# Where the output weights, the first pair's weights and the output operands of a hybrid flow step are made

## The chip, the cores and the metric

One core of one Trainium2 chip runs the whole step. The metric is the device time in microseconds. The core has five engines: PE (TensorE, matmul), DVE (VectorE), ACT (ScalarE), POOL (GpSimd) and SP, which here only issues DMAs. POOL issues some DMAs too. Each engine works through its own queue in order; semaphores order the engines against each other.

## The reference, cut to what matters

There is one layer and two groups of tokens: 2048 sample tokens and 128 prompt tokens, `D_MODEL` = 1024.

```
def mixer(xn, w_in, ..., w_branch, w_out, s0_f, s0_b, grid):
    proj = jnp.einsum('btd,de->bte', xn, w_in)
    qkv, beta, dec, z_a, u_b, v_b, z_b, x_c, z_c, gates = jnp.split(proj, points, axis=-1)
    qkv = short_conv(qkv, conv_w)
    ...
    br = jnp.stack([o_a, o_b, o_c], axis=2)          # delta scan, spatial gating, Fourier mix
    pb = jnp.einsum('btnw,nwd->btnd', br, w_branch)
    gt = jax.nn.sigmoid(gates.reshape(B, T, N_BRANCH, D_MODEL))
    merged = jnp.einsum('btnd,btnd->btd', gt, pb)
    return jnp.einsum('btd,de->bte', merged, w_out), s_f, s_b

def reference(...):
    shift, scale, gate = ada_mod(c, w_ada[l], b_ada[l])
    ...
    h = h + gate * out                               # then a final rmsnorm
```

## The kernel before

Tokens lie along the free axis, channels on the partitions. A value that a matmul reads is held as a pair of f16 halves, a high and a low part, after scaling by a power of two; a product then takes three matmuls (high·high, high·low, low·high). Making such a pair (`as_pair`, L933 to L935, or `converting`, L305 to L330) takes a scaled copy on ACT for the high half and a multiply and subtract on DVE for the low one. The scale comes from a sum of squares: ACT squares and sums along the free axis, DVE narrows that to bf16, PE sums it over the partitions with a matrix of ones (`wscb`), and DVE makes the exponent with integer operations (L279 to L281). `mm` (L251) issues every matmul, so nearly all of PE's work has this one line.

The step runs in stages. The framework puts the instructions of each engine in order by priorities and a simulation of its own; `tc.high_priority` and `tc.issue_after` influence it.

1. From the start to about 190 us the tokens are normed and turned, and the normed tokens xh and xl stay in SBUF.
2. From about 190 to 490 us, the conv stage: twelve tiles of 128 qkv columns, each a product over blocks of up to 512 tokens (L1011 to L1025), then a three-tap convolution in three long DVE operations over 2178 columns (L1031 to L1033), SiLU and a store. Beside it run the decays of the delta scan (L923, L924 on DVE), paced, and a generator `beside`, three steps of it after each 512-token block. `beside` first makes the `token_sums`, sums and differences of quarters of the normed tokens as f16 pairs, stored to DRAM for the last merge; then `out_w`: for each of four pairs of column blocks of the output matrix it squares, scales and splits the blocks into f16 pairs `slot` (stored as `wo`), and makes four differences of the blocks (`ot`, on POOL), split likewise and stored as `tw`.
3. From about 500 to 1100 us the scan is prepared and the branches B and C are made.
4. From about 1100 to 1784 us, two merges (`merge`, branches 1 and 2). Per 128 output channels and token block: 24 gate matmuls, 12 branch matmuls, a sigmoid on ACT, products on DVE and, in the second merge, an addition on POOL. The delta scan itself is paced beside them, and so is `gate_rows`: sums for the two residual gate rows, 64 DVE operations (L478, L480) on loads of `w_ada`, stepped by `next(gates, 0)`.
5. From about 1784 to 2047 us, the last merge, of branch 0. It works on pairs of output channel blocks (i and i + 4) and on quarters of the tokens by a scheme of seven products in place of eight, in two passes over the tokens with four pairs each. Its weights come from `pair_weights`: for each pair it loads two blocks of gate weights (`wst`) and the branch weights, squares them in the first pass for the scale, forms differences on POOL, and splits all into `whi`, `wlo`, `bhi`, `blo`. In the second pass all this but the scale is done afresh. `upto(u)` runs the parts that are due at a product u of the pair before. The branch values of branch 0 are `o16`, in a tile named `big`, [128, 2, 4, 2176] f16, loaded in f32 pieces `st` and split. Each pair's merged rows are also turned into seven-fold operands of the output product and stored to DRAM (`paD`, tile `pa` in pool `orp`, L1929).
6. From about 2047 us, the output products: the prompt's (`whole`), then eight pairs of token tiles (`two_tiles`), also with seven products for eight, each on an operand `pa` of 1792 KB loaded from `paD` and on the weights `wo` and `tw`, which lie in the space of xh and xl by then. The loads stand on SP behind each other by `in_turn` (L2182).

Pools matter at two places. The pool `orp` of the last merge is opened where the pools of the merges are closed, and the pool of the output stage where `orp` is closed; a tile in the new pool waits for all that used the space before. `wp` holds the weights in work: two tiles `wst`, four each of `whi` and `wlo`.

Of the kernel before, what the change touches and what calls it, by code (L numbers as in the profile page):

```python
# [20 lines left out]
P = 128  # L21
D = 1024
# [173 lines left out]
def hybrid_flow_kernel(ctx: ExitStack, tc: tile.TileContext, x_prompt, x_sample, state_delta, c, c_ctx, w_ada,  # L196
# [48 lines left out]
    newest, gated_, queued = [None], [None], [False]  # L245
# [59 lines left out]
    def converting(w, st, nkt, cols=P, hi=None, lo=None, tag="w", bufs=5, nth=0):  # L305
# [13 lines left out]
        sb16 = widened(ss, wp, "wsc")  # L319
        if wnext[0] < 11:  # L320
            yield
        s, inv = scales(None, wp, "wsc", sb16)
        w.inv = sb(wp, [P, 1], "winv", bufs=10)
        if isx is None:
            w.own = inv
        else:
            V.tensor_mul(w.inv, inv, isx)
        yield
        w.made = A.activation(w.hi, st, AF.Copy, scale=s)
        w.low = V.scalar_tensor_tensor(w.lo, st, s, w.hi, ALU.mult, ALU.subtract)  # L330
# [612 lines left out]
    q4 = slice(0, 4), slice(4, 8)  # L943
    tp = pool(a1, "tp", 1, side="right")
# [22 lines left out]
    def out_w():  # L967


        for j in range(4):  # L970
            sts = [sb(tp, [P, KT, P], "osts", bufs=2) for _ in range(2)]
            for st, i in zip(sts, (j, j + 4)):
                SY.dma_start(st, w_outb[i].rearrange("p (k c) -> p k c", c=P))
            yield 1
            yield 1
            yield 1
            ss = sb(tp, [P, 2], "oss2", bufs=2)
            for i in range(2):
                A.activation(sb(tp, [P, KT, P], "slot", F16, bufs=4), sts[i], AF.Square, accum_out=ss[:, i:i + 1])
                yield 1  # L980
            sb16 = sb(tp, [P, 1], "oss2b", BF16, bufs=2)
            V.tensor_add(sb16, ss[:, 0:1], ss[:, 1:2])
            yield 1
            s, inv = scales(None, wp, "wsc", sb16)
            for i in (j, j + 4):
                V.tensor_copy(winv[:, i:i + 1], inv)
            yield 1

            def put(dst, src):
                slot = sb(tp, [P, 2, 4, P], "slot", F16, bufs=4)  # L990
                as_pair(slot[:, 0], slot[:, 1], src, s)
                SY.dma_start(dst, slot.rearrange("p l k c -> p l (k c)"))
# [12 lines left out]
    def one_by_one(*gens):  # L1005
        for gen in gens:
            yield from gen
# [1407 lines left out]
```

## Time and profile before

| | us |
|---|---|
| median of three runs | 2244.32 (2244.15 to 2245.19) |
| the profiled execution | 2239.06 |
| its span | 2237.3 |
| PE busy | 2085.7 |
| DVE busy | 1493.8 |
| ACT busy | 1115.0 |
| POOL busy | 978.7 |

The span is what the profile shows from the first instruction to the last; the profiled execution's own time is 1.8 us longer. Busy times count instructions in work. A row of a group shows the line, the engine, the operation, what it writes and reads, its count, then its busy time and mean, and behind the second bar the idle time of its engine just before it with what ended it. PE's clock is shown as a share of full speed; after a long pause matmuls run slower for a while, and the row shows it.

### The profile page before, as it was taken

The page shows a single profiled execution, that of the slowest core. Times are in us where ns is not written, and L with a number is a line of the kernel's source. Part 1 is how long each engine was busy: PE and PEld are TensorE (multiplying, and loading weights), DVE is VectorE, ACT ScalarE, POOL GpSimd, SP SyncE. Part 2 cuts the span into 40 slices and gives each one's busy share as a digit, 9 for nine tenths or more (in the row PEclk, how much of TensorE's full clock was granted, in tenths as well). Part 3 has the DMA queues.
Part 4 walks back from the last instruction along what each step waited for, and adds up shares of the span by engine and source line. Part 5 has one row for each costly group of instructions (what it writes and reads, how often), then busy time and mean ns, then how long its engine had stood idle before and what let it go on. Part 6 is the DMA issues. An engine that isn't in the chain of part 4 may idle for free.

```text
span 2237.3 us, 43354 instructions
## 1 busy us (share of the span) xinstructions
PE 2085.7 (93%) x16169; PEld 1192.7 (53%) x16169; DVE 1493.8 (67%) x3056; ACT 1115.0 (50%) x2545; POOL 978.7 (44%) x1170
## 2 busy tenths in 40 slices
PE   8998888989999999989899999999999889996997
PEld 4454434445555587668556555555555445442443
DVE  6669996668876776665765566766654376885345
ACT  5554655656565564354544445655554354442112
POOL 0345664444565655533422223354452246553364
PEclk9999989999999999999999999999999999998999
DMA  8534864547777574343655556767654743842862
GB/s 351 198 107 135 258 238 145 200 136 231 248 249 243 181 237 119 85 136 112 199 178 168 162 180 189 239 217 222 213 182 154 244 160 135 299 141 110 331 226 85
DMA packets 250467, 427.54 MB, mean 191 GB/s; under 512 B 46200, under 2 KB 133008, under 8 KB 247184
## 3 DMA queue, kind: packets, MB, share of 16 engines
q1 hardware_dynamic: 197744, 323.68, 45.0%
q0 software_dynamic: 12688, 57.04, 6.8%
q10 hardware_dynamic: 39824, 44.05, 5.9%
q8 instruction: 127, 2.08, 0.4%
q14 instruction: 84, 0.69, 0.1%
HBM read 273.46 MB, written 151.22 MB: 190 GB/s over the span
## 4 chain that ended last, share of the span: by engine, by line
PE 42%; DVE 10%; DMA 8%; issue 4%; ACT 4%; POOL 3%; SPq 0%; ACTq 0%; POOLq 0%; DVEq 0%
PE b L251 41%; DMA st<-br 2%; DMA wst<-in_w_blk_dram 1%; DMA wst<-in_w_ada_dram 1%; DVE pa L935 1%; DMA br<-o 1%; POOL E L1201 1%; DVE XB L1200 1%; DMA ei<-XB 1%; DVE wlo L935 1%; DMA pa<-pa 1%; DMA N<-n 1%; DVE wlo L330 0%; POOL mr L2080 0%; DVE big L1786 0%
## 5 line engine op out<-in xcount | busy, mean ns | idle before, releaser
L251 PE MATMUL b<-xh,wlo 128*128 128x512 f16 (+2 forms) x1792 | 599.8, 347 | 17.0 <-DVE wlo L330 17.0
L251 PE MATMUL b<-xh,whi 128*128 128x512 f16 (+2 forms) x1792 | 602.5, 347 | 6.6 <-ACT sg L2090 3.1
L251 PE MATMUL b<-xl,whi 128*128 128x512 f16 (+2 forms) x1792 | 603.0, 347 | 0.0
L251 PEld LDWEIGHTS <-whi 128*128 128x128 f16 x3872 | 348.7, 98 | 334.4 <-issue 24.8
L251 PEld LDWEIGHTS <-wlo 128*128 128x128 f16 x1936 | 189.7, 98 | 200.0 <-DVE wlo L330 18.7
L251 PE MATMUL b<-big,bhi 128*128 128x512 f16 (+1 forms) x960 | 253.2, 350 | 2.9 <-ACT big L1785 1.2
L251 PE MATMUL b<-big,blo 128*128 128x512 f16 (+1 forms) x480 | 163.2, 348 | 0.0
L251 PEld LDWEIGHTS <-xh 128*128 128x128 f16 x1512 | 119.5, 98 | 34.0 <-issue 4.4
L251 PEld LDWEIGHTS <-bhi 128*128 128x128 f16 x960 | 86.9, 98 | 90.5 <-issue 18.2
L1201 POOL TENSOR_TENSOR E<-E,XB 128x31 f32<-128x31 f32 (+15 forms) x155 | 94.3, 609 | 77.3 <-DVE XB L1200 62.0
L1274 POOL COPY T<-ES 32x256 f16<-32x256 f16 x68 | 31.3, 460 | 202.5 <-DMA ES<-ei 193.2
L251 PE MATMUL b<-xh,pa 128*128 128x512 f16 x376 | 100.7, 383 | 20.1 <-DMA pa<-pa 20.1
L251 PEld LDWEIGHTS <-pa 128*128 128x128 f16 x648 | 63.8, 99 | 98.4 <-issue 23.3
L251 PE MATMUL b<-whi,xh 128*128 128x128 f16 x544 | 93.7, 220 | 2.0 <-DVE sg L1542 2.0
L251 PE MATMUL b<-whi,xl 128*128 128x128 f16 x544 | 93.6, 220 | 0.0
L251 PE MATMUL b<-wlo,xh 128*128 128x128 f16 x544 | 93.6, 220 | 0.0
L1825 POOL TENSOR_TENSOR mrow<-mrow,sg 128x512 f32<-128x512 f32 (+1 forms) x40 | 48.4, 1210 | 83.0 <-DVE sg L1824 62.6
L1381 POOL TENSOR_TENSOR skn<-skn,ed 128x512 f32<-128x512 f32 x34 | 37.1, 1090 | 107.9 <-DMA skn<-kv 94.9
L1037 POOL TENSOR_TENSOR cy<-cy,raw 128x545 f32<-128x545 f32 (+1 forms) x48 | 65.1, 1382 | 43.6 <-ACT raw L1036 43.6
L1200 DVE TENSOR_TENSOR XB<-XB,E 128x31 f32<-128x31 f32 (+15 forms) x155 | 54.6, 353 | 41.8 <-POOL E L1201 40.9
L251 PEld LDWEIGHTS <-xl 128*128 128x128 f16 x824 | 74.5, 98 | 14.4
L251 PE MATMUL b<-xl,pa 128*128 128x512 f16 x272 | 77.2, 382 | 0.0
(565 smaller groups left out, 4825.3 us busy)
## 6 DMA issues: line engine op xcount, KB each, us to landing
wst<-in_w_blk_dram SPq DMA_DIRECT2D x66, 512.0 KB, 4.3
pa<-pa POOLq DMA_DIRECT2D x16, 896.0 KB, 4.5
pa<-pa SPq DMA_DIRECT2D x8, 1792.0 KB, 7.7
qkv<-cy POOLq DMA_DIRECT2D x12, 1089.0 KB, 4.9
st<-br SPq DMA_DIRECT2D x48, 256.0 KB, 3.3
dc<-dec SPq DMA_DIRECT2D x17, 512.0 KB, 4.4
kq<-qkv SPq DMA_DIRECT2D x34, 256.0 KB, 5.1
kv<-tok POOLq DMA_DIRECT2D x17, 512.0 KB, 5.2
```

What stands on the lines that cost most here:

```text
L251: newest[0] = PE.matmul(out, l, r, start=start, stop=stop, skip_group_check=reopened)
L935: V.scalar_tensor_tensor(lo, src, s, hi, ALU.mult, ALU.subtract)
L1037: G.tensor_tensor(y[:, c0:c1], y[:, c0:c1], raw[:, 1 + c0:1 + c1], ALU.mult)
L1200: V.tensor_tensor(t3, X3[:, 0:k, k:k + 1].to_broadcast([P, k, n_]), E3[:, k:k + 1, k:32].to_broadcast([P, k, n_]), ALU.mult)
L1201: G.tensor_tensor(E3[:, 0:k, k:32], E3[:, 0:k, k:32], t3, ALU.subtract)
L1274: G.tensor_copy(T16[rows(a0, b), :, :, b], ES[0:32, :, 2 * a0 + b, :, wT])
L1381: G.tensor_tensor(h3(kn_), h3(kn_), bc(ed[:, d, t, :], P), ALU.mult)
L1825: G.tensor_tensor(mr, mr, sg, ALU.add)
```

## The change

- `out_w` leaves the conv stage. It is now a generator `weights_out` stepped in the merges: after each token block from the second channel block of the first merge on (`step=`), and in `norm_step` in the second. It has a pool of its own (`wop`), makes the block differences in place, and takes its squares behind the newest gate product's sigmoid.
- In `token_sums` the splits are a plain copy on ACT and a subtraction, in turn on POOL and on DVE. Each block now advances it by two steps.
- `urgently()` puts the parts of a weight conversion at high priority during the conv stage.
- `gate_rows` leaves the merges for the second pass of the last merge, every second product of its first three pairs.
- The first pair's weights of the last merge are begun in the second merge's last channel block, a part after each token block (`due_`), in the pool `wq`, which is not that of the merges. It was `orp`.
- In the first pass each pair's converted halves are stored to DRAM (`wgD`, `wbD`); in the second they are loaded (`stored`) and not made again.
- The output operands no longer have three buffers. Operands 0, 3, 6 lie in token columns 1024 to 1920 of `o16`, 1, 4, 7 in columns 0 to 896, and 2 and 5 in a tile `pa`. The first is loaded after the second pass's first pair, when that pass works on the other tokens. The sums `tw` are loaded in the last pair.

On PE, around the end of the second merge, before (`bsums` and `wscb` are summed over the partitions for the scales of branch weights and of gate weights; `whi` and `bhi` are high halves of gate and branch weights):

```order
L251 MATMUL b_23758<-big_14010,bhi_23329 128x128
L251 LDWEIGHTS blo_23330
L251 MATMUL b_23758<-big_14010,blo_23330 128x128
L251 LDWEIGHTS ones_2_89
L251 MATMUL b_23817<-bsums_2925_23815,ones_2_89 128x27
...
L251 MATMUL b_23847<-wscb_23845,ones_2_89 128x1
L251 LDWEIGHTS bhi_23873
L251 MATMUL b_24045<-big_14010,bhi_23873 128x512
...
L251 MATMUL b_24155<-big_14010,bhi_23873 128x512
```

The sum for the first pair's scale stands behind all of the merge, and branch matmuls follow it. The same place now, with the row of that sum ahead of it:

```order
L254 MATMUL b_23539<-big_13781,blo_23213 128x512
...
L254 MATMUL b_23556<-wscb_23554,ones_2_89 128x1
L254 LDWEIGHTS whi_23154
L254 MATMUL b_23578<-xh_94,whi_23154 128x512
...
L254 MATMUL b_23672<-big_13781,blo_23213 128x128
L254 LDWEIGHTS ones_2_89
L254 MATMUL b_23739<-bsums_2910_23737,ones_2_89 128x27
L254 LDWEIGHTS whi_23620
L254 MATMUL b_23789<-xh_94,whi_23620 128x64
...
L254 MATMUL b_23789<-xl_95,whi_23620 128x64
```

That sum has moved up 146 rows, into the merge, and gate products follow `bsums`. On SP, the loads at the passage from the last merge to the output, before (`room` holds rows of x, `tw` the weight differences):

```order
L2165 DMA wst_26262<-gate 128x1024
...
L2182 DMA room_26274<-in_x_prompt_dram 128x512
L2182 DMA pa_3208_26283<-pa 128x4x1792
L2182 DMA xh_94<-tw 128x4x1024 x2
L2182 DMA xl_95<-tw 128x4x1024
L2182 DMA room_26274<-in_x_sample_dram 128x1024 x2
L2182 DMA xl_95<-tw 128x4x1024
L2182 DMA pa_3209_26291<-pa 128x4x1792
```

The first operand stands behind the first use of `room`. And now, with the load of the first operand from the second pass:

```order
L2200 DMA big_13781<-pa 128x4x896 x2
...
L1935 DMA whi_26034<-wg 128x512
L1935 DMA wlo_26035<-wg 128x512
L2190 DMA xh_94<-tw 128x4x1024
L2190 DMA xl_95<-tw 128x4x1024
L2190 DMA xh_94<-tw 128x4x1024
L2190 DMA xl_95<-tw 128x4x1024
L2190 DMA room_26261<-in_x_prompt_dram 128x512
L2190 DMA room_26261<-in_x_sample_dram 128x1024 x2
L2190 DMA big_13781<-pa 128x4x896 x2
```

The first operand and `tw` have moved ahead of `room`; the second operand follows it.

```diff
+    def urgently():
+        return tc.high_priority() if urgent[0] else ExitStack()
...
-        with behind_gate():
+        with behind_gate(), urgently():
             w.squared = A.activation(w.lo, st, AF.Square, accum_out=ss)
...
                     st = sb(ep, [P, 2, cn], "st", F16, bufs=3)
-                    as_pair(st[:, 0], st[:, 1], f, 1.0)
+                    A.copy(st[:, 0], f)
+                    (V if i % 2 else G).tensor_tensor(st[:, 1], f, st[:, 0], ALU.subtract)
                     SY.dma_start(sD[p_][:, i, :, k, :], st)
...
-    beside = one_by_one(token_sums(), out_w())
+    beside = token_sums()
...
-                    for _ in range(3):
+                    for _ in range(2):
                         next(beside, 0)
...
-    big = pool(ms_, "big", 1)
+    big = pool(ctx, "big", 1)
     bwp.append(pool(mr_, "bwp", 1))
+    wop = pool(mr_, "wop", 2)
...
-                if each is not None or db > 3:
-                    next(gates, 0)
...
+    def out_w():
+        for j in range(4):
...
+            ss = sb(wop, [P, 2], "oss2")
+            for i in range(2):
+                with tc.issue_after(gated_[0].ins):
+                    A.activation(sb(wop, [P, KT, P], "slot", F16), sts[i], AF.Square, accum_out=ss[:, i:i + 1])
+                yield 1
...
+            b11, b21, b12, b22 = [st[:, q] for st in sts for q in halves]
+            for q, out, x, y in ((0, b11, b12, b11), (2, b12, b22, b12), (1, b22, b22, b11), (3, b21, b21, b22)):
+                G.tensor_tensor(out, x, y, ALU.subtract)
+                yield 1
+                put(tD[q, :, j, :].rearrange("p (l x) -> p l x", l=2), out)
...
-    inv_ = merge(1, True, inv_, then=(2, 20))
+    inv_ = merge(1, True, inv_, then=(2, 20), step=lambda db: next(weights_out, 0) if db else 0)
...
+            wq_.append(pool(last_s, "wq", 1, side="right"))
             sums_in(1)
+            cur.append(pair_weights(0, False))
...
+    due_ = [9, 6, 5, 4, 3, 1]
+
     def norm_step(db):
-        if db > 1 and early:
+        if db == KT - 1:
+            cur[0].upto(due_.pop())
+        if next(weights_out, 0):
+            return
+        if early:
...
+        def stored(self, i):
+            pair = lambda: [sb(wp, [P, KT, P], n_, F16, bufs=4) for n_ in ("whi", "wlo")]
+            ...
+            for due, w_, names in ((3, 0, ("b11", "t2")), (5, 1, ("b21", "t3")), (8, 2, ("t1", "t4")), (10, 3, ("b22",))):
+                yield due
+                ts = pair()
+                for l in range(2):
+                    SY.dma_start(ts[l][:, 0:4 * len(names)], wgD[i, w_, l][:, 0:512 * len(names)].rearrange("p (k c) -> p k c", c=P))
...
+            def keep(w_, ts, nk=KT):
+                for l in range(2):
+                    SY.dma_start(wgD[i, w_, l][:, 0:nk * P], ts[l][:, 0:nk].rearrange("p k c -> p (k c)"))
...
+    def own(i):
+        if i % 3 == 2:
+            return operands(opa, "pa")
+        t0 = (1024, 0)[i % 3]
+        return o16[:, :, :, t0:t0 + 7 * P].rearrange("p l k (n c) -> p k l n c", c=P)
...
     for n_, (p_, i) in enumerate(order):
         nxt = pair_weights(order[n_ + 1][1], n_ > 2) if n_ < 7 else None
...
+            if 3 < n_ < 7 and u % 2 == 0:
+                next(gates, 0)
+            if n_ == 7 and u == 0:
+                gates_in()
+            if n_ == 7 and u in (4, 6):
+                for q in ((1, 0), (2, 3))[u == 6]:
+                    sums_of(q)
...
+        if nxt is not None:
+            nxt.upto(99)
...
+        if n_ == 4:
+            next_pair()
...
     in_turn(x_left, xp_[0:P, left])
-    next_pair(in_turn)
-    sums_of(1)
-    sums_of(2)
-    sums_of(0)
     ahead_rows = two_rows(firsts[0], in_turn)
-    sums_of(3)
     next_pair(in_turn)
```

More of the change, by code (lines that the diff above doesn't have):

```diff
@@ L942, in hybrid_flow_kernel @@
     winv = sb(cp, [P, KT], "winv8")
-    q4 = slice(0, 4), slice(4, 8)
-    tp = pool(a1, "tp", 1, side="right")
+    halves = slice(0, 4), slice(4, 8)
+    urgent[0] = True
     def token_sums():
@@ L1894, in hybrid_flow_kernel @@
     inv_ = merge(2, False, inv_, finish_delta, then=(0, 17), step=norm_step)
-    for _ in gates:
-        pass
     while wsteps:
@@ L1949, in hybrid_flow_kernel @@
     gp, last_load = [], []
-    halves = slice(0, 4), slice(4, 8)
     bscale = sb(cp, [P, 4 * KT], "bscale")
```

282 lines of the change are left out of this document (146 added, 136 removed).

## The prediction

> **What bounds the kernel now.** I read the page's busy shares first, then PE's waits stage by stage, then the windows of the worst stages, then the timeline around the two longest waits. The page's first part gives the busy time of each engine:
>
> ```profile
> span 2237.3 us, 43354 instructions
> PE 2085.7 (93%) x16169; PEld 1192.7 (53%) x16169; DVE 1493.8 (67%) x3056; ACT 1115.0 (50%) x2545; POOL 978.7 (44%) x1170
> ```
>
> TensorE (PE) is busy for 2085.7 of 2237.3 us. So all that this change can win without removing matmuls is 151.6 us of idle time, and a little of PE's own time where matmuls run at half clock after a wait. The waits of PE by line show where that time is: 350 to 500 us and 250 to 350 us (the conv stage), 1770 to 1840 us (merge 2 to the last merge) and 2035 to 2090 us (the last merge to the output products); columns: line waited for, us in all, times, longest.
>
> ```profile
> PE b L251 <- DVE wscb L265: 7.7, 1, 7.7
> PE b L251 <- DVE oss2b L982: 2.9, 1, 2.9
> ...
> PE b L251 <- DVE wlo L330: 17.0, 3, 6.5
> ...
> PE b L251 <- DVE wscb L1990: 12.2, 1, 12.2
> PE b L251 <- DMA mr<-mrg: 0.8, 1, 0.8
> ...
> PE b L251 <- DMA pa<-pa: 20.1, 1, 20.1
> ```
>
> Two single waits, 12.2 and 20.1 us, and a stage with 27.6 us in three kinds of wait (17.0 + 7.7 + 2.9). The windows (busy us and instruction count of PE, PEld, DVE, ACT, POOL, then granted clock, DMA share, GB/s) show what the conv stage lacks, and that the merges and the last merge have little to give:
>
> ```profile
> 250.00:300.00 50.00, 39.65 (x185) 17.86 (x186) 50.00 (x45) 28.97 (x40) 24.08 (x18) 0.90 0.77 260
> 300.00:350.00 50.00, 43.54 (x231) 20.69 (x230) 40.87 (x64) 28.36 (x51) 31.22 (x41) 0.93 0.54 179
> 350.00:400.00 50.00, 42.27 (x225) 20.16 (x224) 34.31 (x57) 29.39 (x51) 17.89 (x20) 0.90 0.48 163
> ...
> 1500.00:1550.00 50.00, 47.21 (x428) 28.08 (x427) 32.04 (x79) 26.02 (x76) 23.52 (x31) 1.00 0.68 209
> ...
> 1950.00:2000.00 50.00, 50.00 (x233) 22.70 (x232) 43.84 (x55) 23.50 (x36) 25.41 (x21) 1.00 0.40 137
> ```
>
> From 250 to 300 us DVE is busy for all 50.00 us: there DVE is the bound, and PE waits for its low halves (wlo). From 350 us DVE has 15.7 us free and the stage waits for single chains instead.
>
> **Conv stage.** Two things leave it: the whole of out_w, and half of the subtractions of the token sums go from DVE to POOL; and token sums advance two steps per block, not three. The groups of 200 to 500 us (count, busy us, mean ns, idle before), and in the last row what SP's queue waited for at the stores of slot (330 to 480 us):
>
> ```profile
> L935 DVE SCALAR_TENSOR_TENSOR st<-sg,st 128x512 f16<-128x512 f32 (+1 forms) x32 | 21.1, 673 | 7.9 <-ACT st L934 7.9
> L935 DVE SCALAR_TENSOR_TENSOR slot<-ot,wsc,slot 128x512 f16<-128x512 f32 x16 | 14.4, 914 | 11.1 <-ACT slot L934 11.0
> L935 DVE SCALAR_TENSOR_TENSOR slot<-osts,wsc,slot 128x512 f16<-128x512 f32 x16 | 12.9, 857 | 2.1 <-ACT slot L934 2.1
> ...
> L924 DVE TENSOR_TENSOR dc<-dc,cst 128x1024 f32<-128x1024 f32 x8 | 13.5, 1683 | 0.0
> ...
> L924 DVE TENSOR_TENSOR E<-E,cst 128x1024 f32<-128x1024 f32 x3 | 3.6, 1211 | 0.0
> ...
> L957 POOL TENSOR_TENSOR sg<-sg,sg 128x512 f32<-128x512 f32 (+1 forms) x8 | 17.7, 2214 | 10.7 <-DVE sg L956 10.5 <-DVE bnds L1482 0.2
> L1001 POOL TENSOR_TENSOR ot<-osts,ot 128x512 f32<-128x512 f32 x7 | 14.7, 2105 | 5.0 <-DVE slot L935 5.0
> ...
> SPq L992 <- DVE slot L935: 44.3, 18, 17.0
> ```
>
> The gain splits at about 340 us. Before it: half of 21.1 us, 10.6 us, leaves DVE, and the rest is thinner per tile of 128 qkv columns. By the starts of the first conv tap (L1031), such a tile takes 25.2, 31.9 and 26.1 us, in the three that four starts bound; PE's own part, three matmuls for each of eight K tiles and of 4.25 blocks, is 22 us at the 0.216 us between the starts of two warm matmuls of 512 columns (the last two rows, from another stage).
>
> ```profile
> 223.78 2.25 DVE L1031 TENSOR_SCALAR cy<-raw,pc 128x2178 f32<-128x2178 f32 x1
> ...
> 248.95 1.34 DVE L1031 TENSOR_SCALAR cy<-raw,pc 128x2178 f32<-128x2178 f32 x1
> ...
> 280.81 1.34 DVE L1031 TENSOR_SCALAR cy<-raw,pc 128x2178 f32<-128x2178 f32 x1
> ...
> 306.91 2.24 DVE L1031 TENSOR_SCALAR cy<-raw,pc 128x2178 f32<-128x2178 f32 x1
> ...
> 2051.69 0.38 PE L251 MATMUL b<-xh 128*128 128x512 f16 x1
> 2051.91 0.38 PE L251 MATMUL b<-xl,xh 128*128 128x512 f16 x1
> ```
>
> That is 3 + 10 + 4 = 17 us beyond PE's part, the 17.0 of the waits. Moving 10.6 us of DVE work pays at most 10.6 there; the order still puts two or three long conv taps between the parts of one weight conversion, so I take half, 5. After 340 us the 7.7 and 2.9 us go whole if their causes go: oss2b is a row of out_w, and the wscb wait is the last link of a weight load that stands in SP's queue, which stood 44.3 us before stores of slot. I take 10. Together −15, bounds 0 (the chains of 350 us on were not SP's doing, and POOL's new subtractions return the rest) and −28 (all 27.6).
>
> What speaks against it is POOL. The same DVE subtraction of 1024 columns takes 1.21 us in one group above and 1.68 us in another, and POOL's 2.21 us: I read this as the two engines slowing each other. The change puts 16 subtractions on POOL and takes out_w's away (14.7 us for seven of them), so the overlap stays about equal; that is why I give no loss. The Trainium skill, "SBUF — State Buffer", section "Who interferes with whom", states that a DVE instruction with two SBUF inputs contends with a GpSimd instruction that reads SBUF. By it each moved subtraction that meets a DVE tensor_tensor would hand back what it saved, and this term would be −10 rather than −15; the two durations of L924 agree with it.
>
> **Start of the last merge.** Before, the first pair's weights may only be squared when merge 2's pools have been given back: its last merged row (mrow) is stored, then ACT squares, DVE adds, PE sums.
>
> ```profile
> 1783.67 0.18 PE L251 MATMUL b<-bsums,ones 128*128 128x27 bf16 x1
> 1796.00 0.16 PE L251 MATMUL b<-wscb,ones 128*128 128x1 bf16 x1 [12.15 <-DVE wscb L1990]
> 1796.99 2.72 PE L251 MATMUL b<-big,bhi 128*128 128x512 f16 x6 [0.82 <-DMA mr<-mrg]
> ...
> 1792.66 1.06 ACT L1987 ACTIVATE wt<-wst 128x1024 f16<-128x1024 f32 x1 [1.28 <-DMA mrg<-mrow]
> ```
>
> In the changed order of PE, shown with the change, the sum wscb stands 146 rows before bsums, in merge 2, and right behind bsums stand gate products, which need nothing of the branch. So 12.15 + 0.82 us go. The six matmuls at 1796.99 come 0.43 us apart against 0.216 later (2.72 us for six, the last of them overlapping): about 1.3 us of half clock also goes. I take back 1 us for a first wait on the converted block: −13, bounds −14.3 and −10 (a first wait as long as one 512 KB load, 4.3 us; its row stands under C).
>
> **Start of the output.** The first output operand (pa) waits for the pool that the last merge holds, which the last store of pa gives back:
>
> ```profile
> 2052.12 0.38 PE L251 MATMUL b<-xh,xl 128*128 128x512 f16 x1
> 2072.58 0.59 PE L251 MATMUL b<-xh,pa 128*128 128x512 f16 x1 [20.08 <-DMA pa<-pa]
> ...
> 2076.80 0.38 PE L251 MATMUL b<-xl,pa 128*128 128x512 f16 x1
> ...
> 2058.88 4.10 DMA pa<-pa
> ...
> 2063.37 0.33 SPq L2182
> ...
> 2063.75 8.05 DMA pa<-pa
> ...
> 2067.88 3.64 SPq L2182 DMA_DIRECT2D room<-in_x_sample_dram  x2
> ```
>
> In the changed order of SP (shown with the change) the first pair's operand is loaded 47 rows before the sums tw, among the second pass's loads, into a finished token range of the branch operand's buffer; the sums tw stand before room. The first pair of output tiles can follow the prompt's products at once: −20.1, and −2.1 for ten matmuls that start 4.22 us apart from first to last, at half clock, where 2.16 is the warm time. What is late next is the second operand. It still stands behind room, which still waits for the last pa store: at 2063.37. With 0.33 us for room's issue and 3.64 for the two loads of x it is issued at about 2067, and its 8.05 us end at about 2075, its first half some us before. Were nothing else to change, PE would have used up the prompt's part at 2052.3 and the first pair, an eighth of the output's 142.1 us on PE, 17.8, at 2070. So some 4 us of the wait come back; −22 + 4 = −18, bounds −22 (the loads overtake) and −10 (the second operand and x share the bandwidth and take 8 us more).
>
> **Merges and passes.** Added to the merges: out_w, that is 8 squares and 32 conversions on ACT, 32 on DVE at 0.9 us as above, 16 blocks on POOL at up to 2.1 us, 8 loads and 32 stores on SP. Taken away: the gate rows, whose DVE work is
>
> ```profile
> L480 DVE SCALAR_TENSOR_TENSOR sg<-wst,scT,sg 128x256 f32<-128x256 f32 x56 | 26.4, 517 | 11.0 <-DMA wst<-in_w_ada_dram 10.9
> ```
>
> so DVE's sum there is level (14.4 + 12.9 = 27.3 against 26.4), and it is free for a third of that stage. In the second pass the pairs' conversions, 14 loads instead of them, free DVE from its 43.84 of 50 us; PE has 0.0 idle in that window, so this wins nothing. The price is the order of the queues: a store waits on SP for its conversion, with the next loads behind it. Bounds −6 (the idle 2.8 us of a merge window, twice) to +12 (one more wait like that of 12.15); no row stands nearer to one end, so I take the middle, +3.
>
> **Sum.** −15 − 13 − 18 + 3 = −43. The profiled execution took 2239.06 us around its span of 2237.3; that gives 2196, and the three runs shown have their median 5.3 us above it, so 2201. I say 2202.
>
> **Rivals.**
> A. The conv stage gives nothing: POOL's subtractions hold up DVE where DVE is full, or the long taps set the pace in any case. For it: 50.00 of 50 us, and the order, in which weight conversions are still spread between taps. Against: 27.6 us named waits, of which 10.6 hang on out_w alone. 2202 + 15 = 2217; if they give back only the first part's 5, 2207.
> B. It gives all: 2202 − 13 = 2189. For it: DVE has room from 300 us on. Against: the 17.0 us come with a DVE that stays nearly full.
> C. Slower. In the second pass each of four pairs now takes four groups of weights from DRAM through SP's queue, together with gate rows, merged rows and the first operand. The DMA part of the page has a load of this size, 512 KB, at 4.3 us to landing:
>
> ```profile
> wst<-in_w_blk_dram SPq DMA_DIRECT2D x66, 512.0 KB, 4.3
> ```
>
> If SP's first-in order makes every one of the 16 groups late by its whole landing, 16 × 4.3 = 69 us are lost: 2271. It decides from ten of 16 groups, where 43 us are gone. Against: four buffers per half, so a group can be two ahead, and a DMA share of 0.40.
> D. Nothing in the balance: the waits move, the first to the branch's operand (the first six matmuls' big), the second to the second pa, and the conv stage stays as in A. That gives 2244, the change doing what it says without time to show. For it: the last store of pa still releases room at the same moment. Against: by the order only the second operand stands behind it.
>
> **Numbers.** My forecast 0.53, A 0.20, B 0.12, D 0.06, C 0.09. The range goes from below B, at the lower bounds of the two other terms (2189 − 13 = 2176), to the forecast with all three gains at their small ends and the last term at its large one, nearly (2202 + 15 + 3 + 8 + 9 = 2237): 2176 to 2236. It leaves out D and most of C and so some 0.15. A measurement here tells 0.2% (4.5 us) from no change. Faster takes the forecast, A and B, 0.85; within 0.2% D, 0.06; slower C, 0.09.
>
> **What would show it.** Conv: the three waits gone or at most 10 us in 250 to 500 us. Last merge: no wait over 3 us near its start, with gate products right behind bsums. Output: no wait between the prompt's last matmul and the first on an operand, and one of some 4 us on the second operand 18 us later. Merges and passes: PE's waits there as small as before; waits on whi or wlo from DRAM of several us in the second pass would be C. I am wrong if the time is above 2236.

## The result and the profile after

The changed kernel takes 2210.96 us (median of four, 2209.05 to 2213.18), the kernel before 2244.76 us beside it (2244.15 to 2246.48). The ratio is 0.9849, with a 95% interval of 0.9831 to 0.9866: 34 us or 1.5% faster, where 42 us were forecast. The profiled execution has a span of 2207.3 us against 2237.3, 30.0 us less. Its page, part 1, after the change:

```profile
span 2207.3 us, 43369 instructions
PE 2084.7 (94%) x16169; PEld 1194.0 (54%) x16169; DVE 1445.0 (65%) x3000; ACT 1096.3 (50%) x2513; POOL 982.1 (44%) x1178
```

PE does the same work in the same time (2084.7 us against 2085.7), so 29 of the 30 us are idle time of PE. Where they went is read off four marks that both traces have; each is the start of one instruction:

| mark | before, us | after, us | won in the stretch up to it | forecast for it |
|---|---|---|---|---|
| first tap of the last conv tile | 468.40 | 468.21 | 0.2 | 15 |
| sum for the branch scales (bsums) | 1783.67 | 1777.17 | 6.3 | -3, for merges and passes together |
| first matmul of the prompt's output | 2047.16 | 2037.87 | 2.8 | 13 |
| end of the span | 2237.3 | 2207.3 | 20.7 | 18 |

The sum of the forecast, 43, was 13 too high on this scale. Its parts missed by 2.7 to 14.8 us each, two one way and two the other. The main waits of PE in the changed kernel, 150 to 250 us, 250 to 350, 1750 to 1840, 1840 to 2010 and 2030 to 2210 us (us in all, times, longest):

```profile
PE b L254 <- DVE wscb L268: 6.1, 2, 3.4
...
PE b L254 <- DVE wscb L268: 26.9, 4, 10.8
...
PE b L254 <- DVE sg L1789: 2.1, 1, 2.1
PE b L254 <- DVE wscb L1958: 1.3, 1, 1.3
...
PE b L254 <- ACT sg L2128: 3.4, 2, 3.0
PE b L254 <- DVE st L2076: 3.3, 2, 2.8
...
PE b L254 <- DMA big<-pa: 1.6, 2, 0.9
```

Both long single waits are gone, the 20.1 us on an operand nearly whole: 1.6 us are left of it. So are all three waits of the conv stage, 27.6 us, but others of 33.0 us stand before 350 us. They are of a kind of which the kernel before had one of 7.7 us, after 350 us: PE waits for wscb, the narrowed sum of squares of a weight block. After 350 us only 1.1 us are left. The windows show in which half (columns as before):

```profile
200.00:250.00 50.00, 43.92 (x225) 21.25 (x224) 50.00 (x40) 29.40 (x40) 28.62 (x17) 0.93 0.69 237
250.00:300.00 50.00, 37.35 (x203) 17.99 (x202) 50.00 (x42) 30.19 (x40) 37.62 (x26) 0.90 0.67 234
300.00:350.00 50.00, 35.75 (x168) 16.05 (x167) 42.44 (x52) 29.21 (x52) 43.39 (x46) 0.86 0.44 148
350.00:400.00 50.00, 49.09 (x269) 23.78 (x268) 22.39 (x33) 20.34 (x36) 14.49 (x25) 1.00 0.34 118
```

From 350 us PE is nearly full (49.09 of 50 us). Before that it lost what it wins there: 117.0 us busy in 200 to 350 us, against 133.0 before. DVE stays full, and POOL has become busier in 300 to 350 us (43.39 of 50 us, before 31.22).

### The profile page after: what moved, and what is told of

Same layout as the page of the kernel before. It is cut to its first block, busy times and chain, and to the rows that moved or that the text cites. A ratio compares the mean times of both kernels' runs of the same rounds, so it can differ in the third digit from the quotient of the medians.

```text
span 2207.3 us, 43369 instructions
## 1 busy us (share of the span) xinstructions
PE 2084.7 (94%) x16169; PEld 1194.0 (54%) x16169; DVE 1445.0 (65%) x3000; ACT 1096.3 (50%) x2513; POOL 982.1 (44%) x1178
## 4 chain that ended last, share of the span: by engine, by line
PE 59%; DVE 15%; DMA 11%; issue 5%; ACT 4%; POOL 4%; SPq 1%; ACTq 0%; POOLq 0%; DVEq 0%
PE b L254 55%; PE b L183 3%; DMA wst<-in_w_blk_dram 2%; DMA st<-br 1%; DMA wo<-slot 1%; DMA sqk<-qk 1%; DVE xl L183 1%; POOL E L1167 1%; DVE pa L941 1%; PE b L1068 1%; DVE cy L997 1%; DVE st L970 1%; DMA ES<-ei 1%; DVE XB L1166 1%; DVE cy L998 1%
## 5 line engine op out<-in xcount | busy, mean ns | idle before, releaser
L1002 POOL TENSOR_TENSOR cy<-cy,raw 128x545 f32<-128x545 f32 (+1 forms) x48 | 70.1, 1486 | 90.6 <-ACT raw L1001 90.6
L254 PEld LDWEIGHTS <-big 128*128 128x128 f16 x480 | 46.8, 98 | 59.4 <-DMA big<-pa 2.6
L254 PE MATMUL b<-xh,big 128*128 128x512 f16 x280 | 74.8, 379 | 1.6 <-DMA big<-pa 1.6
L960 POOL TENSOR_TENSOR sg<-xh,xl 128x512 f32<-128x512 f16 (+1 forms) x36 | 59.2, 1648 | 35.3 <-DVE st L970 14.9
```

Of the source, the lines that this page charges most:

```text
L254: newest[0] = PE.matmul(out, l, r, start=start, stop=stop, skip_group_check=reopened)
L960: on.tensor_tensor(f, xh[:, kk, ts], xl[:, kk, ts], ALU.add)
L1002: G.tensor_tensor(y[:, c0:c1], y[:, c0:c1], raw[:, 1 + c0:1 + c1], ALU.mult)
```

## The experiments

Each kernel is the changed one with the edit shown, unless another is named. A ratio is to the kernel before, timed beside it on the same chip; the changed kernel has 0.9849 (0.9831 to 0.9866). A difference of 0.001 is 2.2 us, and two ratios tell apart what differs by some 0.0025 or more. "Conv mark" is the start of the last tile's first tap: 468.40 us before, 468.21 after. Five kernels below (m_gates, l_remake2, p0_late, p0_orp, o_late) leave the conv stage as the change made it, and their marks lie between 467.8 and 468.9, so a difference of some us there is more than chance. "First six tiles" is the time from the first tile's first tap to the seventh's.

### The conv stage: subtractions shared with POOL

```diff
-                    A.copy(st[:, 0], f)
-                    (V if i % 2 else G).tensor_tensor(st[:, 1], f, st[:, 0], ALU.subtract)
+                    as_pair(st[:, 0], st[:, 1], f, 1.0)
```

> The changed kernel with the token sums' splits as before: every subtraction on DVE, none on POOL. If POOL's subtractions slow DVE down where it is full (contention theory), the first six conv tiles, 157.1 us in the changed kernel, come back to about 153 as before or below, and the whole is some 4 us faster than the changed kernel. If the sharing helped and something else fills DVE (load theory), about 8 us of DVE work come back to the first half and it takes some 160 to 165, the whole up to 6 us slower.

This is c_dve. Ratio 0.9822 (0.9801 to 0.9843), whose interval overlaps the changed kernel's, span 2197.4 us. The first six tiles take 150.9 us, and the conv mark is at 458.99: 9.2 us earlier. It is the answer of the contention theory, and twice its size. More work on DVE made the stage shorter. Groups of 200 to 340 us, kept apart by size, first of the changed kernel, then of this one (where the taps stand one line earlier):

```profile
L997 DVE SCALAR_TENSOR_TENSOR cy<-raw,pc,cy 128x2178 f32<-128x2178 f32 x6 | 17.6, 2928 | 0.0
L998 DVE SCALAR_TENSOR_TENSOR cy<-raw,pc,cy 128x2178 f32<-128x2178 f32 x5 | 14.3, 2869 | 0.0
L970 DVE TENSOR_TENSOR st<-sg,st 128x512 f16<-128x512 f32 x9 | 11.1, 1244 | 0.0
L966 DVE TENSOR_TENSOR sg<-sg,sg 128x512 f32<-128x512 f32 x4 | 5.5, 1382 | 0.0
L965 DVE TENSOR_TENSOR sg<-sg,sg 128x512 f32<-128x512 f32 x4 | 2.7, 666 | 0.0
...
L970 POOL TENSOR_TENSOR st<-sg,st 128x512 f16<-128x512 f32 x8 | 15.4, 1931 | 7.2 <-ACT st L969 7.2
```

```profile
L997 DVE SCALAR_TENSOR_TENSOR cy<-raw,pc,cy 128x2178 f32<-128x2178 f32 x6 | 17.3, 2884 | 0.0
L996 DVE SCALAR_TENSOR_TENSOR cy<-raw,pc,cy 128x2178 f32<-128x2178 f32 x6 | 15.9, 2647 | 0.0
L941 DVE SCALAR_TENSOR_TENSOR st<-sg,st 128x512 f16<-128x512 f32 x16 | 15.3, 967 | 0.0
L966 DVE TENSOR_TENSOR sg<-sg,sg 128x512 f32<-128x512 f32 x3 | 3.0, 994 | 0.0
L965 DVE TENSOR_TENSOR sg<-sg,sg 128x512 f32<-128x512 f32 x3 | 2.9, 955 | 0.0
```

The means go up in some rows (the splits' subtractions 1244 ns against 967, L966 1382 against 994) and down in others (L965 666 against 955), because each is a mixture of two durations. In both traces every one of the 24 sums of 512 columns on DVE (L962, L965, L966) takes either 0.62 to 0.69 us or 1.51 to 1.66 us, and every long one overlaps work of POOL. So what counts is how many operations POOL's work hits. From 150 us to the seventh tile's first tap, 63 of DVE's 193 operations in the changed kernel last over 0.25 us longer than the shortest of their kind, and 51 of 218 here; each of them overlaps work of POOL. By the same measure DVE loses some 59 us to this in the changed kernel and 48 here, an estimate from the two timelines. That takes back most of what leaves DVE: it is busy 185.3 us of that stretch in the changed kernel and 184.4 here. Besides, it stands idle 23.4 us there in the changed kernel and 15.1 here, mostly waiting for ACT's copies and POOL's sums. POOL also stands in the changed kernel's chain of work that ended last, where it had other work to do for the convolution:

```profile
245.72 6.64 POOL sg L960
252.36 2.16 POOL st L970
254.52 6.77 POOL cy L1002 x4
```

The prediction gave this sharing no loss, because out_w's POOL work left the stage too. But out_w's blocks stood after 340 us, where DVE had room; the subtractions came to stand at 200 to 340 us, where it has none. The Trainium skill, "SBUF — State Buffer", section "Who interferes with whom", says that a DVE instruction with two SBUF inputs contends with a GpSimd instruction that reads SBUF; the two durations of the sums, 0.68 and some 1.63 us, the long one only beside POOL, agree. How the 9.2 us divide between that and the waits for ACT and POOL, no run tells apart.

### The conv stage: the priority of a weight conversion

```diff
-    urgent[0] = True
```

> The changed kernel without high priority for the parts of a weight conversion in the conv stage. If the priority is what made PE wait for scale sums (26.9 us on wscb in 250 to 350 us) in place of low halves (17.0 us before), those 26.9 us fall to under 17 and the first six tiles to 150 or less. If DVE's load is the cause, the wait changes its name only, and the six tiles stay within 3 us of 157.

This is c_calm. Ratio 0.9812 (0.9791 to 0.9833), span 2196.0 us, conv mark at 457.69: 10.5 us earlier. Of the expectation's two sides neither holds whole. The wait on wscb did fall away (26.9 to nothing in 250 to 350 us, where 8.0 us on wlo stand instead, with 9.3 more on wlo in 200 to 250), but the first six tiles take 161.2 us; they start 5 us earlier, and the tiles after them win nearly 10. The taps are DVE's work; PE itself is busy 131.4 of the 150 us from 200 to 350 us, against 117.0 in the changed kernel. What the priority did is seen in PE's timeline of the changed kernel:

```profile
252.17 0.38 PE L254 MATMUL b<-xh,wlo 128*128 128x512 f16 x1
252.38 0.38 PE L254 MATMUL b<-xh,whi 128*128 128x512 f16 x1
263.53 0.16 PE L254 MATMUL b<-wscb,ones 128*128 128x1 bf16 x1 [10.77 <-DVE wscb L268]
263.56 0.59 PE L254 MATMUL b<-xl,whi 128*128 128x512 f16 x1
263.94 0.63 PE L254 MATMUL b<-xh,wlo 128*128 128x512 f16 x1
```

A sum of one column, for a tile to come, stands in the midst of a group of products that have all their operands. PE takes its queue in order, so the whole of PE waits 10.77 us for a DVE cast of 0.14 us that is late behind other DVE work, and then runs at half clock (0.43 us from one start to the next, 0.216 before the wait) until 266.8. "Urgent" moved the sum ahead in PE's queue, and not what it waits for. The squares on ACT end at 253.74 us; the cast starts at 263.34, behind six DVE operations that run from 253.43 us on. These take 10.4 us, all beside work of POOL, where the shortest of their kinds add up to 4.6, so this one wait holds a part of POOL's price too.

### The conv stage: both, and the number of steps

c_only undoes the two and also takes three steps again; of the change's edits to the conv stage, only the removal of out_w is left. c_both leaves two steps.

```diff
-    urgent[0] = True
-                    A.copy(st[:, 0], f)
-                    (V if i % 2 else G).tensor_tensor(st[:, 1], f, st[:, 0], ALU.subtract)
+                    as_pair(st[:, 0], st[:, 1], f, 1.0)
-                    for _ in range(2):
+                    for _ in range(3):
```

> The changed kernel with the conv stage as before in all but the output weights: splits on DVE, three steps a block, no high priority for weight conversions; only the output weights' scaling has left it. By the prediction's term the 10.6 us of waits that hung on them go, and the last first-tap starts at about 458, the whole 8 to 12 us faster than the changed kernel, like each of the two single undoings (459.0 and 457.7 there). If the two undoings add, it starts at about 449 and the whole is 16 to 20 us faster. If both only happened to give a better order, it can be anywhere, 468 too.

> The changed kernel with splits on DVE and no high priority for weight conversions, but the change's two steps a block where the kernel that gave ratio 0.9755 has three. If the number of steps is of no account, the last first-tap starts within 3 us of 448.1 and the ratio is 0.974 to 0.977. If two steps thin the load out, the first six tiles take under 150 us and the ratio is below 0.974; if they only move the order, it can be up to 0.981.

c_only: ratio 0.9755 (0.9738 to 0.9771), 2188.73 us against 2244.42, span 2185.9. It has the lowest ratio of all runs, 21 us below the changed kernel. c_both: 0.9761 (0.9729 to 0.9793). The last first-tap, changed kernel, then c_only:

```profile
468.21 1.36 DVE L996 TENSOR_SCALAR cy<-raw,pc 128x2178 f32<-128x2178 f32 x1 [15.59 <-ACT raw L990]
```

```profile
448.11 1.36 DVE L994 TENSOR_SCALAR cy<-raw,pc 128x2178 f32<-128x2178 f32 x1 [2.17 <-ACT raw L988]
```

So the two undoings add, 9.2 + 10.5 against 20.1: taking the subtractions off POOL is worth 9.2 us with the priority and 9.6 without it (457.69 to 448.1), taking the priority away 10.5 us with them and 10.9 without. The number of steps is of no account (c_both, 447.97). PE's busy time in 200 to 350 us does not add so: 117.0 us in the changed kernel, 129.1 in c_dve, 131.4 in c_calm and 131.2 in c_only.

Removing out_w alone moves the conv mark from 468.40 to 448.11 and so is worth 20.3 us there; the two other edits took 20.1 us of it back. Of the 20.3, 4.2 stand before the first tap (198.58 to 194.40 us), 0.6 in the first six tiles (153.3 to 152.8) and 15.5 after them. PE from 350 us to the mark, before and in c_only:

```profile
350.00:468.40 118.40, 107.80 (x580) 52.07 (x579) 80.73 (x118) 73.62 (x120) 52.18 (x50) 0.94 0.49 171
```

```profile
350.00:448.11 98.11, 98.11 (x553) 48.42 (x552) 43.59 (x57) 45.54 (x70) 27.97 (x37) 1.00 0.27 95
```

The 10.6 us without work are gone, and the granted clock is 1.00 in place of 0.94. In 250 to 350 us the waits are again of the kind and size that they had before:

```profile
PE b L254 <- DVE wlo L336: 17.8, 3, 9.1
```

### The conv stage: token sums later

c_late2 lets the token sums begin in the seventh tile; c_late3 in the fifth, without the priority; c_best in the fourth, without the priority and with all splits on DVE. In all three a step's DVE and POOL work stands behind the newest work of the convolution on that engine.

```diff
+    taps = [None, None]
+
+    def behind_taps():
+        stack = ExitStack()
+        for t_ in taps:
+            stack.enter_context(tc.issue_after(t_.ins))
+        return stack
...
-                if tn == 512 and ct:
-                    for _ in range(2):
-                        next(beside, 0)
+                if tn == 512 and ct > 5:
+                    with behind_taps():
+                        for _ in range(3):
+                            next(beside, 0)
...
+            taps[0] = V.scalar_tensor_tensor(y, raw[:, 2:LP], convw(2, ct), y, ALU.mult, ALU.add)
...
+                taps[1] = G.tensor_tensor(y[:, c0:c1], y[:, c0:c1], raw[:, 1 + c0:1 + c1], ALU.mult)
```

> The changed kernel with the token sums begun in the seventh conv tile, each step behind the newest convolution tap on DVE and the newest product of the convolution on POOL, three steps a block. The load theory (decays, taps and token sums together fill DVE and POOL in the first six tiles, while DVE is busy 22 of 50 us after 350 us) expects the first six tiles at PE's 22 us each, 133 to 142 us in place of 157, the later six at most 5 us longer, and the whole 10 to 20 us faster than the changed kernel, about 2193 to 2200. If single chains bound the tiles (chain theory), it is within 4 us of the changed kernel.

> The changed kernel with the token sums begun in the fifth conv tile, behind the newest convolution work, three steps a block, and without the high priority of weight conversions. The load theory expects fewer than 12 us of waits in 200 to 350 us and fewer than 8 us after, and the whole 6 to 15 us below the 2202 us that begin in the seventh tile gave; the rival, that the token sums cost the same wherever they stand, expects it within 4 us of that.

> The changed kernel with the token sums begun in the fourth conv tile, behind the newest convolution work, splits on DVE, no high priority for weight conversions. The contention theory (a subtraction on POOL costs DVE as much as it saves) with the load theory expects fewer waits than beginning in the fifth tile with splits on POOL gave, and a ratio to the kernel before of 0.973 to 0.979. If sharing with POOL is neutral, 0.979 to 0.982.

Ratios 0.9835 (0.9809 to 0.9860), 0.9793 (0.9777 to 0.9810) and 0.9816 (0.9797 to 0.9834). In c_late2 the first six tiles take 139.1 us and start 20 us earlier, as the load theory expects; then four of the five tiles with the sums take 27 to 31 us each, and the conv mark is at 458.9. c_late3 has it at 459.0, c_best at 460.6. The work of the sums does not vanish in DVE's free time after 350 us: beside the taps it makes PE wait there. The load theory holds for where the waits are and not for the sum. c_late3's ratio is 9 us below c_late2's, as was expected, but not for the reason given: its conv mark is the same, and PE stands idle 17.3 us in 200 to 350 us and 15.2 from there to the mark, where under 12 and under 8 were expected. c_best's ratio lies in the range of the rival, that sharing with POOL is neutral. With the sums late, the price of the two edits does not show: c_late2, which keeps both and begins three tiles later, has its mark 1.7 us before c_best, which has neither. So the prices above hold for sums that begin early. c_best is 14 us slower than c_only, which differs only in when the sums begin and in their not standing behind the taps; which of these two costs the 14 us, no run tells apart. In 250 to 350 us c_best and c_late3 wait 15.2 and 16.8 us for wscb, and after 350 us once more 12.2 and 15.0, without any priority: a sum ahead of its cast on PE can come from the order alone.

### The merges: gate rows

In m_gates the gate rows are stepped in the merges again, with their old buffer; the steps in the second pass go.

```diff
+                if each is not None or db > 3:
+                    next(gates, 0)
...
-            acc = sb(wq_[0], [P, 512], "wt2").rearrange("p (g c) -> p g c", g=2)
+            acc = sb(ep, [P, 512], "sg", bufs=4).rearrange("p (g c) -> p g c", g=2)
...
-            if 3 < n_ < 7 and u % 2 == 0:
-                next(gates, 0)
```

> The changed kernel with the gate rows back in the merges, where they were before, beside the output weights. If taking them from the merges paid for the 6.3 us by which the stretch from the conv stage to the end of the merges got shorter, that stretch gets 4 to 8 us longer again. If it cost the last merge its time, the last merge gets up to 5 us shorter. If neither, the whole stays within 3 us of the changed kernel.

Ratio 0.9942 (0.9921 to 0.9963), span 2226.5 us: 19 us slower than the changed kernel. The conv mark is at 468.36, and bsums comes 15.1 us later:

```profile
1792.30 0.18 PE L254 MATMUL b<-bsums,ones 128*128 128x27 bf16 x1
```

The size is double what was expected. With the same conv mark as the kernel before, where bsums comes at 1783.67, this one has the merges 8.6 us longer: the price of out_w there, with the first pair's weights at the end. Taking the gate rows out pays 15.1, and the two together make the 6.3 us of the table. How firm such a difference is shows in two kernels told of below, which have the same work in the merges as each other: bsums comes at 1771.77 in one and at 1781.25 in the other. From the conv mark to bsums, all eleven kernels without gate rows in the merges take 1303.5 to 1313.2 us, the two with them (m_gates and l_remake2) 1323.9 and 1323.6. So 15.1 is clear of what the order alone moves, 6.3 and 8.6 are not. For the last merge the gate rows' presence is not the burden that was supposed. Their 16 matmuls take 4.1 us of PE there, in the changed kernel:

```profile
L254 PE MATMUL b<-wt,sel 128*2 128x256 f32 x16 | 4.1, 378 | 0.0
```

yet the stretch from bsums to the prompt's first matmul takes 264.0 us without them and 260.7 with them.

### The second pass: stored halves

l_remake2, on top of m_gates: the second pass makes its weights afresh, nothing is stored, and the gate loads come two products later.

```diff
-            self.gen = self.stored(i) if again else self.made(i)
+            self.gen = self.made(i, again)
...
-            keep(0, w0)
...
-            for n_, b in enumerate(self.branch):
-                for l in range(2):
-                    SY.dma_start(wbD[i, n_, l], b[l].rearrange("p k c -> p (k c)"))
```

> The kernel with the gate rows back in the merges (m_gates), and besides that without stored halves: the second pass makes the pairs' weights afresh, and nothing of them is written to or read from DRAM. Against m_gates. If the stores and reloads are what costs the last merge some 8 us of its 13 us gain (queue theory), the stretch from the sum for the branch scales to the first output product, 269 us in m_gates, gets 5 to 10 us shorter. If the making afresh costs the same or more (DVE theory: 41 to 44 of 50 us busy there before), it stays within 3 us or gets longer.

Ratio 0.9915 (0.9898 to 0.9933) against m_gates' 0.9942; the intervals overlap. From bsums to the prompt's first matmul 262.4 us against 264.0. So the stores and the 48 reloads neither cost nor win the last merge more than 2 us. The queue theory falls, and with it rival C.

### The start of the last merge: the first pair's weights

p0_late begins the pair after the merges, in a pool of its own beside the last merge's; p0_orp begins it there too, in the last merge's pool.

```diff
-        if db == KT - 1:
-            cur[0].upto(due_.pop())
...
     orp = pool(ms_, "orp", 1)
+    wq_.append(pool(ms_, "wq", 1))
+    cur.append(pair_weights(0, False))
```

```diff
     tmp = sb(orp, [P, D], "sums")
+    wq_.append(orp)
+    cur.append(pair_weights(0, False))
```

> The changed kernel with the first pair's weights begun after the second merge, in a pool in the space of the merges' pools, as before. If the wait of 12.2 us at the start of the last merge was this wait alone, it comes back with 10 to 14 us, and the whole is 8 to 14 us slower than the changed kernel. If most of that gain is lost again later in the first pass whatever the start, the whole is under 5 us slower.

> The changed kernel with the first pair's tiles in the last merge's own pool, opened when the merges' pools are closed, and begun there, as before the change. Before, the squares waited for that space. If that space made the 12.2 us wait, it is back at the start of the last merge with 10 to 14 us, and the whole is 4 to 12 us slower than the changed kernel, since up to 6 us of later waits in the first pass should then shrink. If the squares start without it, as they did with a pool beside it (p0_late: no wait over 3.2 us), the whole is within 4 us of the changed kernel.

p0_late: ratio 0.9869 (0.9852 to 0.9886), 4 us above the changed kernel with overlapping intervals, and the same span, 2207.3 us. p0_orp: 0.9902 (0.9885 to 0.9919), span 2221.9, 12 to 15 us slower. PE at the passage in p0_orp:

```profile
1781.25 0.18 PE L254 MATMUL b<-bsums,ones 128*128 128x27 bf16 x1
1792.86 0.16 PE L254 MATMUL b<-wscb,ones 128*128 128x1 bf16 x1 [11.43 <-DVE wscb L1954]
1793.81 2.72 PE L254 MATMUL b<-big,bhi 128*128 128x512 f16 x6 [0.79 <-ACT bhi L940]
```

It is the old wait, row by row, and ACT's squares are released by the store of the last merged row as they were before:

```profile
1789.52 1.06 ACT L1951 ACTIVATE wt<-wst 128x1024 f16<-128x1024 f32 x1 [1.21 <-DMA mrg<-mrow]
```

In p0_late, whose tiles only lie elsewhere, the longest wait at this place is 3.2 us, where 10 to 14 were expected:

```profile
PE b L254 <- DVE msc L2052: 3.2, 1, 3.2
PE b L254 <- DVE wscb L1954: 3.1, 1, 3.1
PE b L254 <- ACT sg L2126: 3.1, 1, 3.1
```

So what held the pair back before was the space of its tiles. What that wait is worth is less sure than that it is there: from bsums to the prompt's first matmul p0_orp takes 271.5 us, p0_late 266.8 and the changed kernel 260.7, and the rest of p0_orp's loss lies before bsums. That the change begins the pair inside the merge wins some 4 us or nothing.

### The output: the first operand

```diff
-        if n_ == 4:
-            next_pair()
...
+    next_pair(in_turn)
     ahead_rows = two_rows(firsts[0], in_turn)
```

> The changed kernel with the first output operand loaded only in the output stage, behind the first use of room, the rest unchanged. If that load's place is the whole of the 20.7 us that the output stage won, a wait of 15 to 22 us stands before the first product on an operand and the whole is 16 to 22 us slower than the changed kernel. If the order of tw and room counts too, the wait is 5 to 14 us.

This is o_late. Ratio 0.9909 (0.9894 to 0.9925), span 2221.9 us: 14 us slower than the changed kernel. The wait is back:

```profile
2057.30 0.61 PE L254 MATMUL b<-xh,big 128*128 128x512 f16 x1 [16.30 <-DMA big<-pa]
```

16.3 us and not the 20.1 us of before: some 4 us came from elsewhere. Two things differ that no run tells apart: the operand is now two transfers, and the tw loads no longer follow right behind it. From the prompt's first matmul to the end this kernel takes 186.2 us against 169.4 in the changed one, 16.8 more; the cost of the whole, 14 us, is a little below that and below what was expected.

## Why the prediction was right or wrong, step by step

**The time** lies in the range, and between the forecast and rival A. That is in part luck: two terms were some 10 and 15 us too hopeful, two others 9 and 3 us too cautious, and the range was 60 us wide.

**Conv stage, forecast -15, measured -0.2.** The step that failed is "the overlap stays about equal; that is why I give no loss". The subtractions on POOL cost 9.2 us and the priority, to which the prediction gave no term at all, 10.5. The 5 us taken before 340 us for the moved subtractions were thus a loss. The removal of out_w was undersized: 10 us were taken for it, after 340 us, and it gave 20.3, 15.5 of them in the tiles after the sixth. The cause was the right one, since from 350 us on c_only's PE never waits. But the sum counted only the waits there and not the half clock that comes with them, which it did count in its two next terms: at a granted clock of 0.94 over 118.40 us, 0.06 x 118.40 is some 7 us, an estimate and at most that. Where the 4.2 us before the first tap come from stays open. Before 350 us c_only's 17.8 us of waits are those of before (17.0). Rival A named the outcome and one of its causes, POOL; its other, the long taps, no run tested. The bounds, 0 to -28, held.

**Merges, forecast within +3, measured -6.3.** The measured time lies just below the bound of -6. "DVE's sum there is level" was read as no gain. Level it is, 422 us against 418 from 1080 us to bsums, but the two loads are not alike to PE: with out_w the merges are 8.6 us longer, and the gate rows had cost 15.1. Of these 4.1 us are their own matmuls, which the prediction overlooked; they went on to be paid in the last merge. Of the rest, 11 us, some 7 are idle time of PE: from 1080 us to bsums it stands idle 31.3 us in m_gates and 24.4 in the changed kernel. They lie in many small waits in both; which of them the gate rows cause stays open, and so does what the last 4 are.

**Start of the last merge, forecast -13, measured -2.8 over the whole last merge.** The mechanism was right and p0_orp shows it: 11.43 + 0.79 us of waits return when the space is shared. What failed is "I take back 1 us for a first wait". In the changed kernel PE waits 10.5 us in the last merge (on sg, st and wscb), before it was 4.4 us beside the long wait, and it has the 4.1 us of gate matmuls more: -12.15 - 0.82 - 1.3 + 6.1 + 4.1 is -4.1, within 1.3 us of what was measured. The waits of PE before, from 1800 to 2040 us, and then the groups with the new ones, from 1777 to 2038 us of the changed kernel:

```profile
PE b L251 <- ACT sg L2090: 3.1, 4, 1.5
PE b L251 <- DVE st L2038: 1.3, 2, 1.0
```

```profile
L254 PE MATMUL b<-ts,whi 128*128 128x512 f16 (+1 forms) x288 | 64.1, 322 | 3.7 <-DVE st L2076 3.7
L254 PE MATMUL b<-xh,whi 128*128 128x512 f16 (+1 forms) x192 | 55.7, 317 | 5.5 <-ACT sg L2128 3.4 <-DVE sg L1789 2.1
```

They stand behind DVE and ACT. One would think that the long wait had given these engines time to get ahead. The runs hardly bear it out: p0_orp, which has the wait again, has some 6 us of waits on sg (L2126) and st (L2074) in the last merge, where the changed kernel has 7.1 on the same two and the kernel before 4.4. Why these waits came stays open.

**Output, forecast -18, measured -20.7.** Right: by o_late the operand's place is worth 16.8 us in this stage and 14 in the whole; the rest was not taken apart. The second operand was expected 4 us late and is 1.6 us late. PE also comes to it later than was reckoned: the 142.1 us leave out the products of L183, and with them an eighth is 147.4 / 8 = 18.4 us; the first pair took 19.0, with 0.6 of a wait. Room is issued 15.65 us after the first matmul of the prompt, before 16.2; after it the two loads of x take 0.89 us on SP, where 3.64 were taken from the crowded queue of before:

```profile
2053.52 0.34 SPq L2190 DMA_DIRECT2D room<-in_x_prompt_dram  x1
2053.92 0.89 SPq L2190 DMA_DIRECT2D room<-in_x_sample_dram  x2
2054.86 1.08 SPq L2190 DMA_DIRECT2D big<-pa  x2
```

**Rivals.** B did not occur. c_only, at 2188.7, is at B's 2189, but not by B's mechanism: 17.8 us of the waits that B removes are still there, and the merges and the output gave more than was forecast. C fell by l_remake2, and in the changed kernel PE has no wait on whi or wlo from DRAM. D's conv half occurred, its two moved waits did not.

## What to carry to other kernels

Read an edit that raises the priority of a small step by the queue that it enters: on an engine that works in order it holds up all that is ready behind it until its input comes (10.77 us here), so the input must be early first. Work moved from a full engine to its neighbour must be priced in the stretch in which it will stand, by the durations that both engines have there when they overlap, and not by totals of a stage. And a change of many parts wants each part undone alone: this one won 34 us, with 20 more lost to two of its edits.

## What the runs showed of the hardware that was not expected

That one PE instruction of 0.16 us can cost 10.77 us and 1.5 us of half clock, with all other operands there, was not expected. And POOL's work lengthens a DVE operation in a step and not in proportion to its size: in the conv stage of these traces most operations that are hit last some 0.8 to 1.1 us longer, 1.63 us in place of 0.68 at 512 columns, 2.17 in place of 1.21 at 1024 and 3.37 in place of 2.48 in a tap of 2178. Not every operation beside POOL's work is hit, but in the six traces looked through (before, changed, c_dve, c_calm, c_only, c_both) none was lengthened by over 0.25 us without it.
